# Forward substitution one hop later, up-weight loads and output stores on the sync queue, and the up-weight copies tied behind the output copies

## The chip, the cores and the metric

The kernel runs on one core of one Trainium2 chip. The metric is device time in microseconds; the kernel before was timed three times, with a median of 1085.12 us (1085.11 to 1085.61). Five engines work side by side: TensorE (PE, matmuls, with its weight loads shown as PEld), VectorE (DVE), ScalarE (ACT), GpSimd (POOL) and SyncE (SP), which issues most of the DMA transfers. ACT can issue transfers too; such issues stand in ACT's own instruction order.

## The reference

One layer of a decoder trunk on 512 tokens of width 2048:

```
h = RMSNorm(x);  z = h @ W_in          # r,k,v,decay and rate inputs | gate | pool input | pool gate
w = exp(-exp(-softplus(-(w0 + tanh(wd) @ W_up)) - 0.5));  a = sigmoid(a0 + ad @ A_up)
S_t = S_{t-1} (diag(w_t) - kk_t^T (a_t * kk_t)) + v_t^T k_t;  y_t = S_t r_t    # 16 heads of 64
y = GroupNorm per head (y) + bonus;  pool = windowed means, per-group linear map
x += concat(y, pool) * SiLU(gate) @ W_out
x += sigmoid(x @ W_pg + b_pg) * (p @ W_ple);  out = RMSNorm(x)
```

All in float32. The kernel reaches that accuracy with TensorE's float32r format by splitting each operand into a high part and a remainder and doing three matmuls (high x high, low x high, high x low) in `mm3` (L157).

## The kernel before, in words

**Dense work.** Weights come in 256 KB blocks: SP loads `raw_*`, ACT copies it to `whi_*` (L132), DVE subtracts to get `wlo_*` (L133). Blocks of columns give `zk`, `zr`, `zv`, `zg` (one per head pair) and `zb` (pool). These matmuls form a long stream that `pump` hands out in units of three; they fill TensorE between the small matmuls of the recurrence. After the stage of head pairs follow W_out (`acc_o`), the gate and the embedding (`acc_g`), and the last norm.

**Head pairs.** The 16 heads are treated as 8 pairs j of 128 columns, and the 512 tokens as 8 chunks of 64. The main loop does, for each j, `prepare(j+1)`, `recur(j)` and `gather(j+1)`.

- `decay_and_rate(j)` (L519) is called at the start of `gather(j-1)`. It takes the raw up-weights ur and ar, which `load_ab(j)` (L347, transfers at L354) has loaded, and makes PE's operands: ACT copies ur to us (L524) and its other half to uaz (L525), DVE subtracts to put the remainder in half of us (L526), and the same for as. PE then does pu and pa, whose results ACT turns into sig and tha. Each of us, as and uaz is one buffer, used again for the next j.
- `prepare(j)` builds the tiles ar and bk on DVE and stores bk to DRAM (bkd, L610). At its start it calls `load_ab(j+1)`. `scores(j)` does the chunk products (pm, masked to mt) and a bonus term (pbo, from kph and kpl), sends a part of mt to DRAM (nd, L651), reads it back as n (L656) and gathers bk as bg (L662).
- `invert(j)` (L668) is forward substitution in 31 steps of two DVE instructions, tm (L674) and an addition into xw (L678). The first step waits for n. At the end SP stores xw (xd, L682) and loads it back as x (L689).
- `recur(j)` runs the 8 chunks in 23 hops. A hop is a matmul, a DVE or ACT result (zs, uv, sbd) and some dense units. `step()` counts the hops; beyond hop HS it draws HN steps of `invert(j+1)` and ties them behind the last of these DVE results (`lead`). `between` stands after chunk 0 and holds `scores(j+1)`. After the last chunk, 32 small py<-uv,mt matmuls end the outputs, and ACT copies py to ysb (L847). DVE then takes statistics of ysb (L862, L864) and starts a reciprocal root with ve (L867) and rs (L143).
- The output yo is multiplied by the gate sg and stored to yd by ACT's queue (L893); the pool group's sgp goes the same way (L438).

**What sets the order.** PE's order in this stage is that of the program text. The order on DVE, ACT, SP and POOL is worked out by a scheduler with its own costs when the program is built; `tc.issue_after(x)` ties what follows it behind instruction x, and `tc.high_priority` moves an instruction up. At run time each engine goes through its list in that order.

With HS = 5 and HN = 2 the 31 steps fall on hops 6 to 20, two each, the last on hop 21, where the xd stores are issued too.

Of the kernel before, what the change touches and what calls it, by code (L numbers as in the profile page):

```python
# [21 lines left out]
NJ = DR // P  # L22
# [12 lines left out]
def trunk_kernel(ctx: ExitStack, tc: tile.TileContext, x, p, norm_g, w_in, mu, w0, w_up, a0, a_up,  # L35
                 k_k, k_a, r_k, ln_w, ln_b, w_pool, pool_scale, w_out, w_ple, w_pg, b_pg, final_g, out):
    nc = tc.nc
    PSUM = bass.MemoryType.PSUM
    x, p, w_in, w_out, w_ple, w_pg = x[0], p[0, 0], w_in[0], w_out[0], w_ple[0], w_pg[0]
    out = out[0]  # L40
# [146 lines left out]
    yd = dram.tile([KT, P, T], F32, name="yd", bufs=1)  # L187
# [5 lines left out]
    n_ = 0  # L193
# [154 lines left out]
    def load_ab(j):  # L348
        jc = slice(j * P, (j + 1) * P)
        w2 = []  # L350
        for nm, src in (("u", w_up), ("a", a_up)):
            raw = rw.tile([P, P], F32, name=f"{nm}r{j}", tag=f"l{nm}r")
            for h in range(2):
                nc.scalar.dma_start(out=raw[64 * h:64 * h + 64, :], in_=src[0, :, jc])  # L354
            w2.append((raw, rw.tile([P, P], F32R, name=f"{nm}s{j}", tag=f"l{nm}s")))
        wab[j] = w2

# [47 lines left out]
    def pool_unit(n):  # L405
        g, i = n // 4, n % 2
        win = WINDOWS[g]
        ps = psA.tile([P, T], F32, name=f"zb{n}", tag="acc")
        yield from zcols(ps, f"b{n}")
        if n % 4 < 2:  # L410
            u_ = pp.tile([P, T], F32, name=f"u{n}", tag="u")
            nc.scalar.copy(u_, ps)
            s_ = u_
            w_ = 1
            while w_ < win:
                n_ = pp.tile([P, T], F32, name=f"sw{n}_{w_}", tag="sw")
                nc.vector.tensor_tensor(n_[:, w_:T], s_[:, w_:T], s_[:, 0:T - w_], ALU.add)
                nc.vector.tensor_copy(n_[:, 0:w_], s_[:, 0:w_])
                s_, w_ = n_, 2 * w_
            nc.vector.tensor_tensor(s_[:, 0:win], s_[:, 0:win], rc[g], ALU.mult)  # L420
            nc.vector.scalar_tensor_tensor(u_, s_, 1.0 / win, u_, ALU.mult, ALU.subtract)
            if i == 0:
                dhl[g] = (pp.tile([P, 2, T], F32R, name=f"dh{g}", tag="dh", bufs=1),
                          pp.tile([P, 2, T], F32R, name=f"dl{g}", tag="dl", bufs=1))
            dh, dl = dhl[g]
            split(dh[:, i, :], dl[:, i, :], u_)
            return
        dh, dl = dhl[g]
        sgp = pp.tile([P, T], F32, name=f"sgp{n}", tag="sgp", bufs=1)
        silu2(ps, sgp)  # L430
        pq = psM.tile([P, T], F32, name=f"pp{n}", tag="m")
        wh, wl = chunk(f"wp{n}", 0)
        for k in range(2):
            mm3(pq, wh[:, k, :], wl[:, k, :], dh[:, k, :], dl[:, k, :], k == 0, k == 1)
            yield 0
        m = 2 * g + i
        nc.vector.scalar_tensor_tensor(sgp, pq, dp(73, m), sgp, ALU.mult, ALU.mult)
        nc.scalar.dma_start(out=yd[NJ + m], in_=sgp)  # L438

    phl, pn = [], []  # L440

# [74 lines left out]

    H1, H2, H3, H4, H5, HE = 6, 12, 20, 8, 13, 40

    def decay_and_rate(j):  # L519

        (ur, us), (ar_, as_) = wab.pop(j)
        for raw, st, z_, lo, hi in ((ur, us, uaz[0], slice(64, 128), slice(0, 64)),
                                    (ar_, as_, uaz[1], slice(0, 64), slice(64, 128))):
            nc.scalar.copy(st, raw)  # L524
            nc.scalar.copy(z_[hi, :], raw[hi, :])  # L525
            nc.vector.tensor_tensor(st[lo, :], raw[lo, :], st[lo, :].bitcast(F32), ALU.subtract)  # L526

        ps = psM.tile([P, T], F32, name=f"pu{j}", tag="m")
        mm(ps, us, uhh, start=True, stop=False)
        mm(ps, uaz[0], lal, start=False, stop=True)  # L530
        sig = rw.tile([P, T], F32, name=f"sig{j}", tag="t", bufs=4)
        nc.scalar.activation(sig, ps, AF.Tanh, scale=0.5, bias=dp(81, j))
        nc.vector.tensor_scalar(sig, sig, 0.5, 0.5, ALU.mult, ALU.add)
        nc.vector.tensor_tensor_scan(sig, seg, sig, 0.0, ALU.mult, ALU.add)
        pw = rw.tile([P, NCH, C + 1], F32, name=f"pw{j}", tag="pw", bufs=2)
        ipw = rw.tile([P, NCH, C], F32, name=f"ipw{j}", tag="ipw")
        nc.gpsimd.memset(pw[:, :, 0:1], 1.0)
        sig3 = sig.rearrange("p (c t) -> p c t", t=C)
        nc.scalar.activation(pw[:, :, 1:C + 1], sig3, AF.Exp, scale=-KAPPA)
        nc.scalar.activation(ipw, sig3, AF.Exp, scale=KAPPA)  # L540


        ps = psM.tile([P, T], F32, name=f"pa{j}", tag="m")
        mm(ps, as_, ahh, start=True, stop=False)
        mm(ps, uaz[1], lal, start=False, stop=True)
        tha = rw.tile([P, T], F32, name=f"tha{j}", tag="tha")
        nc.scalar.activation(tha, ps, AF.Tanh, scale=0.5, bias=dp(25, j))
        pws[j] = (pw, ipw, tha)
# [28 lines left out]
    def prepare(j):  # L577
        k_, r_, v_ = need("k", j), need("r", j), need("v", j)
        pw, ipw, tha = pws.pop(j)
        kk = kks.pop(j)  # L580
        if j + 1 < NJ:
            load_ab(j + 1)


        ar = rw.tile([P, NCH // 2, 4, C], F32, name=f"ar{j}", tag="ar", bufs=2)
        bk = rw.tile([P, NCH // 2, 4, C], F32, name=f"bk{j}", tag="bk")
        k4 = kk.rearrange("p (q c t) -> p q c t", c=2, t=C)
        pw4 = pw.rearrange("p (q c) t -> p q c t", c=2)
        i4 = ipw.rearrange("p (q c) t -> p q c t", c=2)
        kp = rw.tile([P, T], F32, name=f"kp{j}", tag="kp")  # L590
        nc.vector.tensor_scalar(kp, tha, dp(33, j), dp(41, j), ALU.mult, ALU.add)
        nc.vector.tensor_tensor(kp, kp, k_, ALU.mult)
        nc.vector.tensor_scalar(tha, tha, 0.5, 0.5, ALU.mult, ALU.add)
        nc.vector.tensor_tensor(ar[:, :, 0::3, :], r_.rearrange("p (q c t) -> p q c t", c=2, t=C),
                                pw4[:, :, :, 1:C + 1], ALU.mult)
        nc.vector.tensor_tensor(bk[:, :, 0::3, :], kp.rearrange("p (q c t) -> p q c t", c=2, t=C), i4, ALU.mult)
        nc.vector.scalar_tensor_tensor(ar[:, :, 1:3, :], k_.rearrange("p (q c t) -> p q c t", c=2, t=C), dp(89, j),
                                       pw4[:, :, :, 0:C], ALU.mult, ALU.mult)
        nc.vector.tensor_tensor(kk, kk, tha, ALU.mult)
        made = nc.vector.tensor_tensor(bk[:, :, 1:3, :], k4, i4, ALU.mult)  # L600
        with tc.issue_after(made.ins):
            nc.vector.scalar_tensor_tensor(kp, r_, dp(49, j), kp, ALU.mult, ALU.mult)
            if gates:
                gates.pop()()
        kph = rw.tile([P, T], F32R, name=f"kph{j}", tag="t", bufs=4)
        kpl = rw.tile([P, T], F32R, name=f"kpl{j}", tag="t", bufs=4)
        split(kph, kpl, kp)

        bkd = dram.tile([P, NCH * P], F32, name=f"bkd{j}", tag="bkd")
        nc.sync.dma_start(out=bkd, in_=bk.rearrange("p q s c -> p (q s c)"))  # L610
        st_[j] = dict(pw=pw, ar=ar, bk=bk, bkd=bkd, v_=v_, kp=(kph, kpl))
# [8 lines left out]
    def scores(j):  # L620
# [26 lines left out]
        for par in range(2):  # L647
            pb = 64 * (1 - par)
            for b in range(2):
                rows = slice(pb + 32 * b, pb + 32 * b + 32)  # L650
                nc.sync.dma_start(out=nd[par, b].rearrange("u r c -> r u c"),  # L651
                                  in_=mt[rows, par, :, 1 - par, 32 * b:32 * b + 32])
        nb = []
        for i in range(2):
            t_ = rw.tile([P, 16, 32], F32, name=f"n32{j}_{i}", tag=("kk", "kp")[i])
            n_ = nc.sync.dma_start(out=t_, in_=nd[:, :, :, 16 * i:16 * i + 16, :].rearrange(  # L656
                "a b u r c -> (a b u) r c").unsqueeze(0).to_broadcast([4, 32, 16, 32]))
            nb.append(t_)
        bg = rw.tile([P, NCH, 4, 32], F32, name=f"bg{j}", tag="bk")
        with tc.issue_after(n_.ins):  # L660
            for q in range(4):
# [105 lines left out]
    def recur(j, work, between):  # L767
        d = st_.pop(j)
        pw, ar, mt, bv, uv, mv, x1 = (d[n_] for n_ in ("pw", "ar", "mt", "bv", "uv", "mv", "x1"))
        hop = [0]  # L770
# [4 lines left out]
        def step():  # L775
            hop[0] += 1
            if hop[0] > HS:
                with tc.issue_after(lead[0].ins):
                    for _ in range(HN):
                        next(work, None)  # L780


        ysb = rw.tile([P, NT, P], F32, name=f"ysb{j}", tag="t", bufs=4)
        pys = {}
        for ch in range(NCH):
# [47 lines left out]
            if ch == NCH - 1:  # L833
                for c0 in range(0, NCH, 4):
# [9 lines left out]
                    py4 = py.rearrange("p (s c) -> p s c", c=P)  # L844
                    for pr in range(2):
                        yr = slice(64 * pr, 64 * pr + 64)
                        nc.scalar.copy(ysb[yr, c0 // 2:c0 // 2 + 2, :], py4[yr, pr::2, :])  # L847
            step()
            if ch == 0:
                between()  # L850
# [31 lines left out]
        def finish():  # L882
# [7 lines left out]
            def gate_out():  # L890
                nc.vector.tensor_tensor(yo, yo, bv, ALU.add)
                nc.vector.tensor_tensor(yo, yo, sg, ALU.mult)
                nc.scalar.dma_start(out=yd[j], in_=yo)  # L893

            return gate_out

        pending.append(finish)

    HC, HT, HX = (6, 9, 9), 130, 13
    HS, HN = 5, 2  # L900
    HP = 1000
    pending, normed, gates = [], [], []
    need("k", 0)
# [308 lines left out]
```

## Time and profile before

| what | value |
|---|---|
| timed runs, median | 1085.12 us (1085.11 to 1085.61) |
| profiled execution, its own time | 1082.7 us |
| its span | 1081.0 us, granted clock 0.998 |
| TensorE busy | 1056.6 us |
| DVE / ACT / POOL busy | 714.0 / 441.5 / 75.0 us |
| bytes moved by DMA | 146.94 MB, 136 GB/s mean |

The times of instructions all come from one profiled execution, which took 1082.7 us, 2.4 us less than the median of the timed runs. A row of a timeline reads: start in us, length in us, engine, line, operation, output tile <- input tiles, shapes, how many instructions the row holds, and in brackets how long the engine stood idle before it and what ended that. A row of a group reads: line, engine, operation, count, then shortest/median/longest in ns and the first and last start. Rows named SPq or ACTq are the issue of a transfer, not the transfer.

### The profile page before, as it was taken

How to read it: one execution, taken by the hardware profiler on the slowest of the kernel's cores; microseconds unless marked ns; L12 is line 12 of the kernel's file. 1: busy time of each engine (PE TensorE's matmuls, PEld its weight loads, DVE VectorE, ACT ScalarE, POOL GpSimd, SP SyncE). 2: the span in 40 equal slices, each digit the busy share in tenths (PEclk: the TensorE clock that was granted, in tenths of full speed). 3: DMA queues.
4: the chain of work that ended last, by engine and by line, in shares of the span. 5: the costliest groups of instructions: out<-in, count | busy, mean ns of one | idle time of the engine just before them, and what ended most of it. 6: DMA issues, size and time to landing. Idle time of an engine off the chain costs nothing.

```text
span 1081.0 us, 17106 instructions
## 1 busy us (share of the span) xinstructions
PE 1056.6 (98%) x5996; PEld 872.1 (81%) x5996; DVE 714.0 (66%) x1851; ACT 441.5 (41%) x901; POOL 75.0 (7%) x180
## 2 busy tenths in 40 slices
PE   5999999999999999999999999999999999999996
PEld 4888878888888887878788788888888888888885
DVE  6676978888779789787887857563432424445356
ACT  7633435335335354353352344553222222333337
POOL 2100010110110100200101201000000000000000
PEclk9999999999999999999999999999999999999999
DMA  7434443342634533434435343774434428355434
GB/s 236 117 115 111 139 116 88 116 120 74 168 88 114 144 89 105 120 89 112 106 91 158 100 129 111 239 243 141 171 121 143 166 98 271 122 182 161 169 98 156
DMA packets 212916, 146.94 MB, mean 136 GB/s; under 512 B 68085, under 2 KB 173150, under 8 KB 212830
## 3 DMA queue, kind: packets, MB, share of 16 engines
q1 hardware_dynamic: 192126, 112.28, 35.9%
q10 hardware_dynamic: 20704, 33.56, 9.4%
q8 instruction: 47, 0.77, 0.3%
q14 instruction: 39, 0.32, 0.1%
HBM read 122.21 MB, written 23.07 MB: 134 GB/s over the span
## 4 chain that ended last, share of the span: by engine, by line
PE 91%; DVE 4%; DMA 3%; ACT 2%; issue 1%; ACTq 0%; SPq 0%; DVEq 0%
PE acc_o L157 16%; PE acc_g L157 16%; PE zb L157 14%; PE zv L157 8%; PE zg L157 8%; PE zr L157 8%; PE zk L157 7%; PE py L157 2%; PE pu L157 2%; PE pple L157 2%; PE pm L157 1%; DMA n<-nd 1%; PE pp L157 1%; PE ps L157 1%; DMA xt<-in_x_dram 1%; PE pmv L157 1%
## 5 line engine op out<-in xcount | busy, mean ns | idle before, releaser
L133 DVE TENSOR_TENSOR wlo_g<-raw_g,whi_g 128x512 fp32r<-128x512 f32 x84 | 57.0, 685 | 74.4 <-ACT whi_g L132 72.3
L157 PE MATMUL zb<-hhi,whi_b 128*128 128x512 f32 x256 | 106.0, 414 | 0.0
L133 DVE TENSOR_TENSOR wlo_o<-raw_o,whi_o 128x512 fp32r<-128x512 f32 x64 | 43.9, 690 | 90.9 <-ACT whi_o L132 90.8
L157 PE MATMUL zb<-hhi,wlo_b 128*128 128x512 f32 x256 | 100.4, 392 | 0.0
L157 PE MATMUL acc_o<-whi_o,ylo 128*128 128x512 f32 x256 | 100.2, 391 | 0.0
L157 PE MATMUL acc_o<-whi_o,yhi 128*128 128x512 f32 x256 | 99.9, 390 | 0.0
L157 PE MATMUL zb<-hlo,whi_b 128*128 128x512 f32 x256 | 99.8, 390 | 0.0
L157 PE MATMUL acc_o<-wlo_o,yhi 128*128 128x512 f32 x256 | 99.7, 389 | 0.0
L132 ACT CAST whi_g<-raw_g 128x512 fp32r<-128x512 f32 x84 | 52.0, 621 | 105.3 <-PE acc_g L157 58.9
L157 PE MATMUL acc_g<-whi_g,x2hi 128*128 128x512 f32 x208 | 81.2, 391 | 0.0
L832 POOL TENSOR_SCALAR s0p<-sbd,pw 64x64 f32<-64x64 f32 x96 | 58.0, 604 | 332.0 <-DVE sbd L825 243.5
L157 PE MATMUL acc_g<-wlo_g,x2hi 128*128 128x512 f32 x208 | 80.9, 389 | 0.0
L157 PE MATMUL acc_g<-whi_g,x2lo 128*128 128x512 f32 x208 | 80.6, 389 | 0.0
L132 ACT CAST whi_o<-raw_o 128x512 fp32r<-128x512 f32 x64 | 39.9, 623 | 96.3 <-PE acc_o L157 96.3
L132 ACT CAST whi_b<-raw_b 128x512 fp32r<-128x512 f32 x64 | 39.7, 621 | 86.7 <-PE zb L157 29.2
L133 DVE TENSOR_TENSOR wlo_b<-raw_b,whi_b 128x512 fp32r<-128x512 f32 x64 | 43.6, 683 | 27.3 <-ACT whi_b L132 27.1
L157 PEld LDWEIGHTS zb<-hhi,wlo_b 128*128 128x128 f32 x256 | 48.0, 188 | 10.9
L678 DVE TENSOR_TENSOR xw<-xw,tm 128x60 f32<-128x60 f32 (+24 forms) x248 | 52.1, 210 | 7.0
L157 PEld LDWEIGHTS acc_o<-wlo_o,yhi 128*128 128x128 f32 x256 | 48.1, 188 | 9.9
L157 PEld LDWEIGHTS acc_o<-whi_o,ylo 128*128 128x128 f32 x256 | 48.1, 188 | 9.8
L157 PEld LDWEIGHTS acc_o<-whi_o,yhi 128*128 128x128 f32 x256 | 48.1, 188 | 9.7
L157 PEld LDWEIGHTS zb<-hhi,whi_b 128*128 128x128 f32 x256 | 48.2, 188 | 8.3
(283 smaller groups left out, 2529.6 us busy)
## 6 DMA issues: line engine op xcount, KB each, us to landing
raw_b<-in_w_in_dram SPq DMA_DIRECT2D x64, 256.0 KB
raw_o<-in_w_out_dram SPq DMA_DIRECT2D x64, 256.0 KB
raw_g<-in_w_pg_dram SPq DMA_DIRECT2D x64, 256.0 KB
raw_k<-in_w_in_dram SPq DMA_DIRECT2D x32, 256.0 KB
raw_r<-in_w_in_dram SPq DMA_DIRECT2D x32, 256.0 KB
raw_v<-in_w_in_dram SPq DMA_DIRECT2D x32, 256.0 KB
raw_g<-in_w_in_dram SPq DMA_DIRECT2D x32, 256.0 KB
bkd<-bk SPq DMA_DIRECT2D x8, 512.0 KB
```

What stands on the lines that cost most here:

```text
L132: nc.scalar.copy(hi, raw)
L133: nc.vector.tensor_tensor(lo, raw, hi.bitcast(F32), ALU.subtract)
L157: i = nc.tensor.matmul(*a, **k)
L678: nc.vector.tensor_tensor(xw[:, 0:n_, s + 1:32], xw[:, 0:n_, s + 1:32], tm[:, 0:n_, 0:w_], ALU.add)
L832: nc.gpsimd.tensor_scalar(s0p[hc, :], nxt[hc, hc], pcn[hc], None, ALU.mult)
```

## The change

Four edits:

1. HS goes from 5 to 6, and hop HE1 = 21 takes three steps. The 31 steps now fall on hops 7 to 20, two each, and three on hop 21; the xd stores are issued at hop 22.
2. `load_ab` and both yd stores go through the sync queue (SP) in place of ACT's.
3. `load_ab(j+1)` is called in `scores(j)`, tied behind the n loads, and no longer at the start of `prepare(j)`.
4. The four ACT copies of `decay_and_rate` are tied behind `tail`, the last ysb copy that has been issued by then. For j = 0 and 1 there is none yet.

```diff
 def load_ab(j):
-                nc.scalar.dma_start(out=raw[64 * h:64 * h + 64, :], in_=src[0, :, jc])
+                nc.sync.dma_start(out=raw[64 * h:64 * h + 64, :], in_=src[0, :, jc])
...
-        nc.scalar.dma_start(out=yd[NJ + m], in_=sgp)
+        nc.sync.dma_start(out=yd[NJ + m], in_=sgp)
...
+    tail = []
+
 def decay_and_rate(j):
-            nc.scalar.copy(st, raw)
-            nc.scalar.copy(z_[hi, :], raw[hi, :])
+            with tc.issue_after(tail[0].ins) if tail else ExitStack():
+                nc.scalar.copy(st, raw)
+                nc.scalar.copy(z_[hi, :], raw[hi, :])
             nc.vector.tensor_tensor(st[lo, :], raw[lo, :], st[lo, :].bitcast(F32), ALU.subtract)
...
 def prepare(j):
-        if j + 1 < NJ:
-            load_ab(j + 1)
...
 def scores(j):
+        if j + 1 < NJ:
+            with tc.issue_after(n_.ins):
+                load_ab(j + 1)
         bg = rw.tile([P, NCH, 4, 32], F32, name=f"bg{j}", tag="bk")
...
 def step():
-                    for _ in range(HN):
+                    for _ in range(HN + (hop[0] == HE1)):
...
-                        nc.scalar.copy(ysb[yr, c0 // 2:c0 // 2 + 2, :], py4[yr, pr::2, :])
+                        tail[:] = [nc.scalar.copy(ysb[yr, c0 // 2:c0 // 2 + 2, :], py4[yr, pr::2, :])]
...
 def gate_out():
-                nc.scalar.dma_start(out=yd[j], in_=yo)
+                nc.sync.dma_start(out=yd[j], in_=yo)
...
-    HS, HN = 5, 2
+    HS, HN, HE1 = 6, 2, 21
```

Three places show how the lists of the engines change. The first is ACT at the end of the recurrence of pair 1, around the pu and pa matmuls of pair 3 (a name's digits are the pair; what follows a last underscore is a buffer number; lines behind the first edits stand four later in the changed file). Before:

```order
L847 COPY ysb1_2614<-py1_0_2615 64x256 x2
L137 CAST kqh3_3320<-kk3_3318 128x512
L847 COPY ysb1_2614<-py1_4_2970 64x256 x2
L132 CAST whi_b2_3_1878<-raw_b2_3_1876 128x512
L369 ACTIVATE sv3_3355<-zv3_3130,dprm_133 128x512
L532 ACTIVATE sig3_3333<-pu3_3330,dprm_133 128x512
L547 ACTIVATE tha3_3345<-pa3_3342,dprm_133 128x512
```

And now:

```order
L851 COPY ysb1_2606<-py1_0_2607 64x256 x2
L137 CAST kqh3_3320<-kk3_3318 128x512
L851 COPY ysb1_2606<-py1_4_2966 64x256 x2
L527 CAST us3_2722<-ur3_2719 128x128
L528 CAST uaz0_570<-ur3_2719 64x128
L527 CAST as3_2726<-ar3_2723 128x128
L528 CAST uaz1_571<-ar3_2723 64x128
L132 CAST whi_b2_3_1871<-raw_b2_3_1869 128x512
L369 ACTIVATE sv3_3355<-zv3_3126,dprm_133 128x512
L535 ACTIVATE sig3_3333<-pu3_3330,dprm_133 128x512
```

The four copies for pair 3 now stand between the second ysb copies and whi_b; before they stood behind the pu and pa of the pair ahead.

The second is DVE at the same place. Before:

```order
L862 BN_STATS st1_3285<-ysb1_2614 128x6 x4
L864 BN_AGGR mvr1_3286<-st1_3285 128x2 x4
L138 TENSOR_TENSOR kql3_3321<-kk3_3318,kqh3_3320 128x512
L867 TENSOR_SCALAR ve81_3304<-mvr1_3286 128x8
L133 TENSOR_TENSOR wlo_b2_3_1879<-raw_b2_3_1876,whi_b2_3_1878 128x512
L143 TENSOR_SCALAR rs81_3303<-ve81_3304 128x8
```

(The two rows of the second half's statistics, which read like the first two, stand between kql3 and ve81.) And now, from the second half's statistics on:

```order
L866 BN_STATS st1_3285<-ysb1_2606 128x6 x4
L868 BN_AGGR mvr1_3286<-st1_3285 128x2 x4
L529 TENSOR_TENSOR us3_2722<-ur3_2719,us3_2722 64x128
L871 TENSOR_SCALAR ve81_3304<-mvr1_3286 128x8
L133 TENSOR_TENSOR wlo_b2_3_1872<-raw_b2_3_1869,whi_b2_3_1871 128x512
L143 TENSOR_SCALAR rs81_3303<-ve81_3304 128x8
L529 TENSOR_TENSOR as3_2726<-ar3_2723,as3_2726 64x128
```

The subtract for us3 stands behind the second aggregate, and that for as3 behind wlo_b and rs.

The third is DVE where the substitution for pair 6 begins, in the recurrence of pair 5. Before:

```order
L799 TENSOR_TENSOR zs0_568<-py5_0_6085,mv5_6033 64x128
L133 TENSOR_TENSOR wlo_r7_3_3580<-raw_r7_3_3577,whi_r7_3_3579 128x512
L674 TENSOR_TENSOR tm6_6224<-i32_116,n326_0_6163 128x31
L370 SCALAR_TENSOR_TENSOR sk7_6230<-zk7_6115,prm_131,sk7_6230 128x511
L678 TENSOR_TENSOR xw6_6223<-xw6_6223,tm6_6224 128x31
L674 TENSOR_TENSOR tm6_6224<-xw6_6223,n326_0_6163 128x30
L678 TENSOR_TENSOR xw6_6223<-xw6_6223,tm6_6224 128x30
L674 TENSOR_TENSOR tm6_6224<-xw6_6223,n326_0_6163 128x29
L678 TENSOR_TENSOR xw6_6223<-xw6_6223,tm6_6224 128x29
L674 TENSOR_TENSOR tm6_6224<-xw6_6223,n326_0_6163 128x28
L678 TENSOR_TENSOR xw6_6223<-xw6_6223,tm6_6224 128x28
L133 TENSOR_TENSOR wlo_v7_0_3586<-raw_v7_0_3583,whi_v7_0_3585 128x512
```

And now:

```order
L803 TENSOR_TENSOR zs0_568<-py5_0_6077,mv5_6033 64x128
L133 TENSOR_TENSOR wlo_r7_3_3572<-raw_r7_3_3569,whi_r7_3_3571 128x512
L370 SCALAR_TENSOR_TENSOR sk7_6223<-zk7_6107,prm_131,sk7_6223 128x511
L678 TENSOR_TENSOR tm6_6238<-i32_116,n326_0_6155 128x31
L682 TENSOR_TENSOR xw6_6237<-xw6_6237,tm6_6238 128x31
L678 TENSOR_TENSOR tm6_6238<-xw6_6237,n326_0_6155 128x30
L682 TENSOR_TENSOR xw6_6237<-xw6_6237,tm6_6238 128x30
L133 TENSOR_TENSOR wlo_v7_0_3578<-raw_v7_0_3575,whi_v7_0_3577 128x512
L829 SCALAR_TENSOR_TENSOR sbd1_567<-ps5_2_6253,pw5_5193,s0p5_1_6209 64x64 x2
```

Two steps in place of four stand ahead of wlo_v7 and of sbd1, and sk7 stands ahead of the first of them. In the list before, sbd1 follows wlo_v7 too.

## The prediction, made before the changed kernel was run

> **What bounds the kernel now.** I began with the page's first table, where TensorE (PE) is busy for nearly the whole span.
>
> ```profile
> PE 1056.6 (98%) x5996; PEld 872.1 (81%) x5996; DVE 714.0 (66%) x1851; ACT 441.5 (41%) x901; POOL 75.0 (7%) x180
> ```
>
> Next I took the table of 60 us windows (columns: window, length, then the busy time of PE, PEld, DVE, ACT and POOL, TensorE's granted clock, DMA share, GB/s), to see where PE is not busy in the head-pair stage, which runs up to about 700 us.
>
> ```profile
> 420.00:480.00 60.00, 59.07 (x326) 48.04 (x325) 46.71 (x156) 24.07 (x53) 8.77 (x14) 1.00 0.44 116
> 480.00:540.00 60.00, 58.02 (x382) 47.72 (x381) 48.94 (x135) 21.44 (x47) 6.50 (x14) 1.00 0.42 108
> 540.00:600.00 60.00, 59.48 (x412) 48.68 (x411) 48.44 (x136) 24.79 (x53) 6.97 (x10) 1.00 0.46 123
> ```
>
> These three windows miss 0.93 + 1.98 + 0.52 = 3.4 us; every other window of the stage misses less than 0.5. The waits view names what PE waited for (total us, times, longest).
>
> ```profile
> PE py L157 <- DVE sbd L825: 1.4, 2, 0.9
> PE px L157 <- issue: 1.1, 1, 1.1
> PE pu L157 <- DVE zs L799: 1.0, 2, 0.6
> PE pbo L157 <- DVE kpl L138: 0.3, 1, 0.3
> ```
>
> Together 3.8 us, about the same hole. A matmul's shown end overlaps the next one, so a stop costs a little more than its idle time. The longest run of dense matmuls in the chain of waits gives the true pitch:
>
> ```profile
> 83.27 10.88 PE zk L157 x48
> ```
>
> 10.88 / 48 = 0.227 us. Start to start against that pitch, the stops between 120 and 700 us sum to about 6.5 us (an estimate from the rows of that stretch). So this stage can give at most 6.5 us, 0.6% of the time, while any new wait in front of PE costs its full length, because PE's order is pinned and it has no spare time to catch up.
>
> **The change part by part.**
>
> *The tied copies (added wait).* `decay_and_rate(j)` makes PE's operand us of two steps: ACT copies ur, then DVE subtracts. Before, both ran some 50 us ahead of their use. Now the four ACT copies stand right behind the two ysb copies of the head pair whose end comes just before the pu matmul, and DVE's subtract stands behind the statistics made from those ysb rows. PE's order there is as before: nine dense matmuls after the last py, then pu. So each place is a race between nine matmuls (9 x 0.227 = 2.0 us) and copy, statistics, subtract. Here is the trace of before at j=3, DVE first, then ACT, then PE:
>
> ```profile
> 254.38 0.36 DVE L864 BATCH_NORM_AGGREGATE mvr<-st 128x2 f32<-128x6 f32 x4
> 254.78 0.17 DVE L867 TENSOR_SCALAR ve<-mvr 128x8 f32<-128x8 f32 x1
> 254.89 0.69 DVE L133 TENSOR_TENSOR wlo_b<-raw_b,whi_b 128x512 fp32r<-128x512 f32 x1
> 255.50 0.16 DVE L143 TENSOR_SCALAR rs<-ve 128x8 int32<-128x8 int32 x1
> ```
>
> ```profile
> 253.08 0.74 ACT L847 COPY ysb<-py 64x256 f32<-64x256 f32 x2
> 254.22 0.62 ACT L132 CAST whi_b<-raw_b 128x512 fp32r<-128x512 f32 x1 [0.39 <-ACT ysb L847]
> ```
>
> ```profile
> 254.21 0.39 PE L157 MATMUL pu<-uhh,us 128*128 128x512 f32 x1
> ...
> 254.66 0.39 PE L157 MATMUL pa<-ahh,as 128*128 128x512 f32 x1
> ```
>
> The subtract, and the pitch of the small ACT copies:
>
> ```profile
> L526 DVE TENSOR_TENSOR us<-ur,us x8: 289/289/290, 40.5 to 474.2; 64x128 fp32r<-64x128 f32 x8
> ```
>
> ```profile
> 187.10 0.30 ACT L525 CAST uaz<-ur 64x128 fp32r<-64x128 f32 x1
> 187.30 0.29 ACT L524 CAST as<-ar 128x128 fp32r<-128x128 f32 x1
> ```
>
> At j=3 the ACT copy of us would run from about 253.85 to 254.15, in time for pu at 254.21. But the subtract takes ve's slot at 254.78 and ends at 255.07; with some 0.06 to the next engine pu starts at 255.13, **0.92 later**. Then pa: the four copies, at 0.2 to 0.3 each, end near 254.87, so whi_b moves from 254.22 to 254.89; DVE, in its new order, runs us, ve, wlo_b (needs whi_b, 255.56 to 256.25), rs (0.1), as (0.27, to 256.64). pa starts at 256.70 instead of 254.66, **2.04 later** in all. j=5 and j=7 have the same rows in both orders: three places at about 2.05.
>
> At j=2 and j=6 the `as` subtract stands right behind ve, with no weight split between:
>
> ```profile
> 181.75 0.39 PE L157 MATMUL pu<-uhh,us 128*128 128x512 f32 x1
> ```
>
> ```profile
> 182.33 0.17 DVE L867 TENSOR_SCALAR ve<-mvr 128x8 f32<-128x8 f32 x1
> ```
>
> ```profile
> 473.27 0.39 PE L157 MATMUL pu<-uhh,us 128*128 128x512 f32 x1
> ```
>
> ```profile
> 473.84 0.17 DVE L867 TENSOR_SCALAR ve<-mvr 128x8 f32<-128x8 f32 x1
> ```
>
> us ends 0.29 after ve's old start: pu at 182.68 (+0.93) and 474.19 (+0.92); as ends about 0.45 later, just behind pa's new place, so **0.97** each. At j=4 a key split and ve stand ahead of us:
>
> ```profile
> 326.87 0.39 PE L157 MATMUL pu<-uhh,us 128*128 128x512 f32 x1
> ```
>
> ```profile
> 327.30 0.66 DVE L138 TENSOR_TENSOR kql<-kk,kqh 128x512 fp32r<-128x512 f32 x1
> ...
> 328.07 0.29 DVE L526 TENSOR_TENSOR us<-ur,us 64x128 fp32r<-64x128 f32 x1
> ```
>
> The subtract keeps its row place, now in front of pu: pu at 328.42, **+1.55**. Added: 3 x 2.05 + 2 x 0.97 + 1.55 = **9.6 us**. The lower end takes only the pu waits, 5 x 0.92 + 1.55 = 6.1 (if whi_b or the copies come sooner); the upper, 11, lets every pa cost as at j=3 (5 x 2.05 would be 10.3) with something on top at j=4.
>
> That DVE does not pass a waiting instruction rests on these rows: at 90.16 a substitution step had idled 5.09 us for its matrix, although whi_r was done at 89.14 and wlo_r, the next in the order, needed nothing else.
>
> ```profile
> 88.52 0.62 ACT L132 CAST whi_r<-raw_r 128x512 fp32r<-128x512 f32 x1 [2.05 <-PE zk L157]
> ```
>
> ```profile
> 90.16 0.19 DVE L674 TENSOR_TENSOR tm<-i,n 128x31 f32<-128x31 f32 x1 [5.09 <-DMA n<-nd]
> ...
> 91.91 0.68 DVE L133 TENSOR_TENSOR wlo_r<-raw_r,whi_r 128x512 fp32r<-128x512 f32 x1
> ```
>
> The Trainium skill says the same ("TensorE: Matmul & The Clock Gate", section "Architectural detail: the array is 16× 32×32, not 1× 128×128"): ACT and DVE queues are strict FIFO and PE may only pull weight loads forward, so neither the subtract nor the dense matmuls behind pu can step over the wait. If DVE could take whatever is ready, the subtract would run before the aggregate, at about 254.4, and j=3 would lose about 0.6 instead of 2.04; by that rule it cannot, and the rows above agree.
>
> *The substitution a hop later.* The steps of `invert` stand in DVE's order, and the first waits for its matrix from DRAM. What queues behind it is sbd, and PE waits for sbd:
>
> ```profile
> 512.26 0.19 DVE L674 TENSOR_TENSOR tm<-i,n 128x31 f32<-128x31 f32 x1 [2.21 <-DMA n<-nd]
> ```
>
> ```profile
> 515.85 0.49 PE L157 MATMUL py<-sbd,ar 128*128 128x128 f32 x2 [0.87 <-DVE sbd L825]
> ```
>
> With two steps instead of four ahead of sbd, two pairs of 0.45 us go from its front, and the shifted-copy row sk moves ahead of the wait: more than 0.87. The two sbd waits (1.4 by the waits view, 1.9 start to start with the smaller ones of their kind) go. The third step in the 15th hop is another pair of 0.4; it lies behind a wait of the same hop and only moves the xd stores, whose data the next head pair wants one hop, some 3 us, later. I price it at 0, bound 0 to 0.5.
>
> *The ACT queue freed.* The yd store and the up-weight loads leave ACT, where the issuing instruction waits for its operand:
>
> ```profile
> 425.17 0.32 ACTq L893 DMA_DIRECT2D yd<-yo  x1
> 425.54 0.60 ACT L373 ACTIVATE sg<-zg 128x512 f32<-128x512 f32 x1 [1.55 <-PE pbo L157]
> ```
>
> ACT then does sg and kph without that block, and the subtract in front of the mask products leaves DVE's list there:
>
> ```profile
> 425.67 0.27 DVE L526 TENSOR_TENSOR as<-ar,as 64x128 fp32r<-64x128 f32 x1
> ```
>
> That shortens the waits for kpl and zs, and perhaps the one at px. I credit 2 us of the remaining 4.6 (6.5 - 1.9), bounds 0 and 4.6. On SP, the store stands between two weight loads that are issued ahead of use; the up-weight issues go behind the n loads, in front of the bg gathers:
>
> ```profile
> L354 ACTq DMA_DIRECT2D ur<-in_w_up_dram x16: 472/496/620, 35.9 to 405.4; - x16
> ```
>
> Four issues at 0.5 to 0.6 are 2.2 us ahead of bg, whose transposed copy is used only when the next head pair starts, tens of us later: 0. Should that cover fail, it costs those 2.2 us once per head pair.
>
> *Sum.* +9.6 - 1.9 - 2.0 = +5.7, taken as **+5.6 us**, with ends 6.1 - 6.5 = -0.4 and 11 - 1.9 = +9.1. The profiled execution took 1082.7 (span 1081.0), so 1088.3 in its terms; the median of the timed runs is 2.4 above it, hence **1090.7**.
>
> **The rivals.**
>
> *R1, it cancels.* The new waits are only the 0.92 of each pu (6.1 in all), and PE's six stops let DVE and ACT run ahead, so that all 6.5 us of old stops vanish. Net -0.4: about 1084.7. For it: while PE stands, the others catch up, and most old stops are below 1 us. Against: the stops at 425 to 430, 486 and 515 us lie tens of us from a pu place, and the lead gained is used up by DVE, which is busy for four fifths of these windows.
>
> *R2, faster.* The chip lets the statistics end sooner than I read, say because the ysb copies follow their py with ACT no longer held by stores: the subtract would have to come 0.9 us sooner. Then the tie costs 0.2 per place, 1.2 in all, and 5.7 of old stops vanish: -4.5, 1080.6. It decides from the point where the second aggregate ends before pu's old start less 0.35. Against: at j=3 the ysb row starts with no idle time noted behind kqh, ACT's own work, and no store is near it. The Trainium skill ("DMA: Bandwidth & Descriptors", section "Issuing engines are not separate DMA queues") says that another issuing engine saves no more than the time of issuing; the 0.5 us issue row above is of that size.
>
> *R3, more is lost.* The late sig and tha push the decay chain, x1 comes a hop late, and no old stop goes: +9.6 and another wait of about 1 us at pq in two head pairs: +11.6, 1096.7. For it: DVE is the engine with the least slack. Against: in every pair PE's own delay of 0.9 or more precedes that place.
>
> **How the numbers follow.** Forecast 0.68, with its own range 1087 to 1093.5; R1 0.14; R2 0.08; R3 0.10. A change below 0.2% (2.2 us) can't be told from none here. Faster by more: R2, 0.08. Same: R1, 0.14. Slower: forecast and R3, 0.78. The range takes the forecast's ends (-0.4 and +9.1) and thereby R1: 1084.5 to 1094.7, leaving out R2 and most of R3.
>
> **What would show it.** In the changed profile PE's waits view should get rows pu <- DVE us of about 0.9 (1.5 at j=4) at six places, and pa <- DVE as of about 1.1 at three; the row py <- DVE sbd should go, and kpl and zs shrink. The windows up to 600 us should each miss 1 to 2 us of PE. If pu has no wait for us, the subtract was not behind the statistics in time and the main term is wrong; if py <- sbd stays, the substitution's term is.

## The result and the profile after

The changed kernel takes 1092.58 us (median of six runs, 1090.85 to 1095.52) beside 1085.2 us for the kernel before in the same runs. The ratio is 1.0067, with a 95% interval of 1.0053 to 1.0081: 5.7 to 8.8 us slower, 7.3 in the middle. The forecast was 1090.7, with a range of 1084.5 to 1094.7. The profiled execution took 1091.91 us with a span of 1090.2, 9.2 us above the profile of before.

First the busy times and then the waits of PE in the profile after:

```profile
PE 1058.1 (97%) x5996; PEld 870.7 (80%) x5996; DVE 716.4 (66%) x1851; ACT 440.0 (40%) x901; POOL 75.1 (7%) x180
```

```profile
PE pu L157 <- DVE us L529: 5.1, 6, 1.4
...
PE pa L157 <- DVE ve L144: 2.4, 3, 0.8
PE py L157 <- DVE sbd L829: 1.6, 4, 0.8
PE pu L157 <- DVE zs L803: 1.0, 3, 0.4
```

PE's work is the same; the span grew by waits. Two rows are new: pu waits for us at six places, pa at three. They are 7.5 us of idle time, 9.0 from start to start, and 9.9 with the matmuls right behind the stops, which come late too (below). The rows for sbd and zs are still there, 1.6 and 1.0 where the profile of before had 1.4 and 1.0.

Here is pair 3's place: ACT, DVE and PE in the profile after.

```profile
255.89 0.30 ACT L527 CAST us<-ur 128x128 fp32r<-128x128 f32 x1
...
256.93 0.62 ACT L132 CAST whi_b<-raw_b 128x512 fp32r<-128x512 f32 x1
```

```profile
256.42 0.36 DVE L868 BATCH_NORM_AGGREGATE mvr<-st 128x2 f32<-128x6 f32 x4
256.81 0.29 DVE L529 TENSOR_TENSOR us<-ur,us 64x128 fp32r<-64x128 f32 x1
257.13 0.17 DVE L871 TENSOR_SCALAR ve<-mvr 128x8 f32<-128x8 f32 x1
257.58 0.69 DVE L133 TENSOR_TENSOR wlo_b<-raw_b,whi_b 128x512 fp32r<-128x512 f32 x1 [0.28 <-ACT whi_b L132]
258.19 0.16 DVE L143 TENSOR_SCALAR rs<-ve 128x8 int32<-128x8 int32 x1
258.26 0.28 DVE L529 TENSOR_TENSOR as<-ar,as 64x128 fp32r<-64x128 f32 x1
```

```profile
256.01 0.40 PE L157 MATMUL zv<-hhi,wlo_v 128*128 128x512 f32 x1
257.15 0.50 PE L157 MATMUL pu<-uhh,us 128*128 128x512 f32 x1 [0.75 <-DVE us L529]
257.49 0.39 PE L157 MATMUL pu<-lal,uaz 128*128 128x512 f32 x1
258.68 0.47 PE L157 MATMUL pa<-ahh,as 128*128 128x512 f32 x1 [0.80 <-DVE ve L144]
...
259.22 0.60 PE L161 MATMUL pv<-ident,sv 128*128 128x128 f32 x4
```

ACT's copy of us is ready at 256.19, but DVE subtracts only after the aggregate, at 256.81, and pu starts 0.05 after its end. The subtract for as follows wlo_b, which has waited for whi_b behind the four copies. The row names ve as what pa waited for; as itself ends at 258.54, just before pa's start.

The second pu starts 0.34 us behind the first, not 0.23, and the second pa 0.31 behind its first. So a stop costs about 0.1 us more than the start of the waiting matmul shows. The whole place is therefore read from the last dense matmul to the first pv behind pa: 256.01 to 259.22 here, 3.21 us. In the profile of before it was 1.15 us:

```profile
253.97 0.40 PE L157 MATMUL zv<-hhi,wlo_v 128*128 128x512 f32 x1
...
255.12 0.60 PE L161 MATMUL pv<-ident,sv 128*128 128x128 f32 x4
```

The stops of PE from start to start, against the 0.227 us pitch:

| place | prediction | profile after |
|---|---|---|
| pu, j=2, 3, 5, 6, 7 | 0.93, 0.92, 0.92, 0.92, 0.92 | 0.92, 0.92, 0.92, 0.92, 0.89 |
| pu, j=4 | 1.55 | 1.55 |
| pa, j=3, 5, 7 | 1.13 each | 0.96, 0.97, 0.96 |
| sum of these, with 0.05 forecast for pa at j=2, 6 | 9.6 | 9.0 |
| whole place, j=2 to 7 in order | 0.97, 2.05, 1.55, 2.05, 0.97, 2.05 | 1.04, 2.06, 1.66, 2.07, 1.03, 2.04 |
| sum of the whole places | 9.6 | 9.9 |
| py for sbd, whole stage | 0.4 left of 2.3 | 2.3 |
| pu for zs, px, pbo | about 2 of 4.2 left | 2.8 |
| W_out, first operand | 0 | 0.56 |

In the table by windows (120 to 180 us and on), the two slices that hold j=3 and j=4 miss 2.4 and 1.4 us of PE, where before they were full:

```profile
240.00:300.00 60.00, 57.62 (x402) 46.79 (x401) 47.01 (x132) 24.67 (x54) 5.89 (x11) 1.00 0.39 106
300.00:360.00 60.00, 58.62 (x409) 48.16 (x408) 52.11 (x157) 26.43 (x58) 9.00 (x12) 1.00 0.41 111
```

So the loss is where it was forecast. The 9.9 us of the six places, the 0.6 at W_out, and the 1.4 that the row pu for zs, px, pbo gave back make 9.1 of the 9.2 us by which the span grew. What did not come is most of the gain. Theories for that: the longer wait of the first substitution step for its matrix n has come with the up-weight loads, now issued right behind n (theory N); or n's time varies anyway (theory V); and ACT was not the limit at the places where its freedom was to pay.

### The profile page after: what moved, and what is told of

Read it like the earlier page. It is cut to its first block, busy times and chain, and to the rows that moved or that the text cites. A ratio compares the mean times of both kernels' runs of the same rounds, so it can differ in the third digit from the quotient of the medians.

```text
span 1090.2 us, 17103 instructions
## 1 busy us (share of the span) xinstructions
PE 1058.1 (97%) x5996; PEld 870.7 (80%) x5996; DVE 716.4 (66%) x1851; ACT 440.0 (40%) x901; POOL 75.1 (7%) x180
## 4 chain that ended last, share of the span: by engine, by line
PE 86%; DMA 5%; DVE 4%; ACT 3%; issue 1%; SPq 0%; ACTq 0%; DVEq 0%
PE acc_g L157 16%; PE acc_o L157 15%; PE zb L157 13%; PE zr L157 8%; PE zv L157 8%; PE zg L157 7%; PE zk L157 6%; PE pple L157 2%; PE py L157 2%; DMA yin<-yd 2%; PE pm L157 1%; PE pu L157 1%; DMA ur<-in_w_up_dram 1%; PE ps L157 1%; DMA xt<-in_x_dram 1%
```

## The experiments

| kernel | median us | ratio to before, 95% interval |
|---|---|---|
| the changed kernel | 1092.58 | 1.0067 (1.0053 to 1.0081) |
| before, tie alone | 1094.52 | 1.0095 (1.0080 to 1.0110) |
| changed, tied behind uv | 1082.07 | 0.9968 (0.9957 to 0.9980) |
| changed, no tie | 1115.97 | 1.0299 (1.0277 to 1.0322) |
| before, HS = 6 alone | 1082.89 | 0.9984 (0.9974 to 0.9993) |
| before, HS = 7 alone | 1080.76 | 0.9957 (0.9943 to 0.9972) |
| changed, no tie, loads behind bg | 1085.82 | 1.0009 (0.9997 to 1.0020) |
| before, yd stores on sync alone | 1086.02 | 1.0002 (0.9991 to 1.0013) |
| changed, no tie, loads in the old place | 1083.03 | 0.9985 (0.9976 to 0.9995) |
| the same with HS = 7 | 1081.66 | 0.9966 (0.9954 to 0.9978) |
| changed, tied behind uv, HS = 7 | 1081.05 | 0.9961 (0.9947 to 0.9976) |

The kernel before lay between 1084.5 and 1085.4 us in these comparisons, so ratios are compared, not medians.

### The tie alone

```diff
 # the kernel before, and
+            with tc.issue_after(tail[0].ins) if tail else ExitStack():
+                nc.scalar.copy(st, raw)
+                nc.scalar.copy(z_[hi, :], raw[hi, :])
...
+                        tail[:] = [nc.scalar.copy(ysb[yr, c0 // 2:c0 // 2 + 2, :], py4[yr, pr::2, :])]
```

> The kernel before with the tie alone: hops, queues and the place of the loads as before. Theory T: pu waits of 0.9 at j=2, 3, 5, 6, 7 and 1.55 at j=4, pa waits of 0.96 at j=3, 5, 7: +9.0 us, near 1094, and the old waits of PE for sbd (1.9 us from start to start at 441, 516 and 590 us) are still there. Rival R1 (the six stops let DVE and ACT run ahead and take the old waits away): +2.5 to +4, 1088 to 1089. Theory Q: no more than half of +9, below 1090.

Measured: 1094.52, 0.95% or 10.3 us above the kernel before (8.7 to 11.9). The waits of PE in its profile:

```profile
PE pu L157 <- DVE us L529: 5.1, 6, 1.4
PE py L157 <- DVE sbd L828: 3.4, 4, 1.6
...
PE pa L157 <- DVE ve L144: 2.4, 3, 0.8
```

The two rows for us and ve are those of the changed kernel to the digit, 9.0 us from start to start and 9.9 for the whole places, and the sbd waits are not smaller: 4.6 us from start to start. R1, by which the six stops let the other engines run ahead and take the old waits away, has fallen.

### The same tie one place earlier

```diff
 # the changed kernel, but
-                    nc.scalar.copy(uv[pb:pb + 64, ch, hc], psu[hc, hc])
+                    u_ = nc.scalar.copy(uv[pb:pb + 64, ch, hc], psu[hc, hc])
+            tail[:] = [u_]
...
-                        tail[:] = [nc.scalar.copy(ysb[yr, c0 // 2:c0 // 2 + 2, :], py4[yr, pr::2, :])]
+                        nc.scalar.copy(ysb[yr, c0 // 2:c0 // 2 + 2, :], py4[yr, pr::2, :])
```

> The changed kernel with the copies tied behind the last chunk's uv copies in place of the ysb copies; all else as changed. DVE's subtracts for us and as now stand ahead of the statistics of ysb. Theory T (the loss is DVE's subtract standing behind these statistics, not the tie as such): no wait of pu or pa, 9.0 us less than the changed kernel: 1083.5, with the sbd waits of PE still near 2 us. Rival (any tie of this kind costs, because four copies of 0.2 us now stand in front of ysb, the key split and the next weight split): PE waits by 0.8 us or more at other places of each pair, and the time stays above 1087.

Measured: 1082.07, 0.32% below the kernel before and 1% below the changed one. The subtracts for pair 3 stand ahead of the statistics (DVE, then PE):

```profile
249.98 0.29 DVE L529 TENSOR_TENSOR us<-ur,us 64x128 fp32r<-64x128 f32 x1
...
250.39 0.28 DVE L529 TENSOR_TENSOR as<-ar,as 64x128 fp32r<-64x128 f32 x1
...
254.63 0.36 DVE L869 BATCH_NORM_AGGREGATE mvr<-st 128x2 f32<-128x6 f32 x4
```

```profile
254.22 0.40 PE L157 MATMUL zv<-hhi,wlo_v 128*128 128x512 f32 x1
254.46 0.39 PE L157 MATMUL pu<-uhh,us 128*128 128x512 f32 x1
```

pu follows the dense matmul by 0.24 us: no wait, at any pair. So the cost is the place to which the tie behind ysb brings the two subtracts, behind the statistics and (for as) behind a weight split that has waited for ACT, and not a tie as such. The difference to the changed kernel is about 10.7 us (1.0067 less 0.9968), beside the 9.9 us of the six places; the intervals of the two ratios are wider than what is left between them.

### No tie at all

```diff
 # the changed kernel, but
-            with tc.issue_after(tail[0].ins) if tail else ExitStack():
-                nc.scalar.copy(st, raw)
-                nc.scalar.copy(z_[hi, :], raw[hi, :])
+            nc.scalar.copy(st, raw)
+            nc.scalar.copy(z_[hi, :], raw[hi, :])
```

> The changed kernel without the tie of the up-weight copies; the sync queue, the loads behind n and the later substitution stay. Theory T (the tie pays all of the loss): the six pu waits and three pa waits of the changed kernel, 9.0 us from start to start, vanish, so about 9 us below the changed kernel, near 1083.5; but the subtracts for us and as now stand between the first substitution steps and sbd, 0.56 us more ahead of sbd, so the sbd waits stay near 2.3 us or grow to 4, which leaves 1083.5 to 1085.5. Theory Q (the moved transfers pay a good part): the wait of the first substitution step for n stays long and the time stays above 1087. Theory S (PE loses the same elsewhere): 1090 or more, with new waits of PE that sum to the old.

Measured: 1115.97, 32 us above the kernel before (30 to 35), the slowest of all, which no theory had. The waits of ACT and of PE show a new one:

```profile
ACT uaz L527 <- DMA ur<-in_w_up_dram: 50.3, 7, 9.2
```

```profile
PE ps L157 <- ACT uv L816: 24.5, 6, 5.5
```

Pair 4's loads, in the recurrence of pair 2 (ACT, then PE):

```profile
309.90 0.30 ACT L527 CAST uaz<-ur 64x128 fp32r<-64x128 f32 x1 [9.18 <-DMA ur<-in_w_up_dram]
...
310.94 0.42 ACT L816 COPY uv<-pu 64x64 f32<-64x64 f32 x2
```

```profile
305.49 0.40 PE L157 MATMUL zk<-hhi,wlo_k 128*128 128x512 f32 x1
311.42 0.80 PE L157 MATMUL ps<-uv,bkn 128*128 128x128 f32 x2 [5.53 <-ACT uv L816]
```

With the loads issued behind n and nothing to hold the copies, the scheduler put the copies ahead of a uv copy, as if the loads had landed. They land 9 to 10 us after their issue, and uv, which PE needs, stands behind them on ACT. So the third edit (later loads) needs a tie of some kind, and my prediction did not see that it would cost some 32 us without one. In the profiled execution, 38 us longer than that of before, the six stops are 25.5 us from start to start; about 13 more (an estimate) are the stretches of 27 us in all behind them in which matmuls came at half pace (last section). The experiment thus doesn't say what the changed kernel is without the statistics' wait; the version tied behind uv does.

### The later substitution alone, and once more later

```diff
 # the kernel before, with
-                    for _ in range(HN):
+                    for _ in range(HN + (hop[0] == HE1)):
-    HS, HN = 5, 2
+    HS, HN, HE1 = 6, 2, 21
 # and the second one with
+    HS, HN, HE1 = 7, 2, (19, 20, 21)      # hop[0] in HE1
```

> The kernel before with the substitution a hop later alone (HS = 6, three steps in hop 21). My step of the prediction: the two large sbd waits go, -1.9 us, 1083.3, and the wait from the second issue of the n loads to the first step stays at its 5.0 to 5.5 us, since no transfer has moved. Rival (the hop does nothing, because the first step is still tied behind the same zs and its wait for n still stands ahead of sbd): the sbd waits stay at about 2 us and the time at 1085.2.

> The kernel before with the substitution one hop later still (HS = 7, three steps in hops 19, 20 and 21), so that the first step stands behind sbd of that chunk, and nothing waits for n ahead of it. Theory: the sbd waits that were left with HS = 6 (1.8 us) go, whatever the time that n takes: 1081, 1.8 us below HS = 6 and 3.5 below the kernel before. Rival (DVE's list is full later: three steps a hop delay zs, sbd or the last step, and with it the next pair's first matmuls): new waits of PE at zs, sbd or pq, 1083 or more.

Measured: 1082.89 (0.8 to 2.8 us less than before) and 1080.76 (3.0 to 6.2 less). By the ratio the first is 1.7 us, beside the 1.9 that were forecast. But its profile doesn't look as expected, since the wait for n stays ahead of sbd:

```profile
587.01 0.19 DVE L674 TENSOR_TENSOR tm<-i,n 128x31 f32<-128x31 f32 x1 [4.14 <-DMA n<-nd]
```

```profile
PE py L157 <- DVE sbd L825: 1.5, 2, 1.2
```

Here n took 7.0 us from the end of its second issue to the first step, where the profile of before had at most 5.5. Hop 7 is tied behind the same zs as hop 6, because `lead` is set only by zs and sbd, and hop 7 is that of a uv copy: a hop later took two steps from in front of sbd and left the first step where it was. With HS = 7 the first step stands behind sbd, and the wait is gone in all seven pairs of the main loop:

```profile
586.61 0.29 DVE L825 SCALAR_TENSOR_TENSOR sbd<-ps,pw,s0p 64x64 f32<-64x64 f32 x1
586.93 0.19 DVE L674 TENSOR_TENSOR tm<-i,n 128x31 f32<-128x31 f32 x1
```

The rival there, new waits at zs or pq, shows little: one stop of 0.66 us at a pq matmul near 410 us, which stands in the HS = 6 profile too.

### The kernel before once more, and the loads behind bg

These two ask why n took so long.

> The kernel before once more, for a second profile. Theory V (the time from the second n issue to the first step varies from one execution to the next by 1 to 2 us in single pairs, whatever stands on the queue): one or more pairs at 5.9 us or above, and with it other sbd waits of PE than the first profile showed. Theory N (the longer times come from the changed queues): all eight pairs again between 4.9 and 5.6 us, and sbd waits at the same three places.

Measured: one execution, 1085.98, a span of 1084.3. The last pair, DVE and then PE, and the row of the waits view:

```profile
589.97 0.19 DVE L674 TENSOR_TENSOR tm<-i,n 128x31 f32<-128x31 f32 x1 [3.69 <-DMA n<-nd]
```

```profile
593.49 0.49 PE L157 MATMUL py<-sbd,ar 128*128 128x128 f32 x2 [1.55 <-DVE sbd L825]
```

```profile
PE py L157 <- DVE sbd L825: 4.1, 5, 1.5
```

n took 6.55 us here and 5.3 to 6.0 at the other pairs; the sbd waits are 4.1 us where the first profile of the same kernel had 1.4. So theory V is right for this kernel: the first profile was an execution in which n came early.

```diff
 # the changed kernel without the tie, and
-        if j + 1 < NJ:
-            with tc.issue_after(n_.ins):
-                load_ab(j + 1)
...
-                nc.sync.dma_start(out=bg[32 * q:32 * q + 32],
+                b_ = nc.sync.dma_start(out=bg[32 * q:32 * q + 32],
...
+        if j + 1 < NJ:
+            with tc.issue_after(b_.ins):
+                load_ab(j + 1)
```

> The changed kernel without the tie, and with the up-weight loads issued behind the bg gathers instead of right behind the n loads. Theory N (the up-weight loads right behind n make n land later, 5.6 to 6.75 us from the second issue where the kernel before has 5.0 to 5.5): the time from issue to first step falls back to 5.0 to 5.5 us, the sbd waits of PE fall below 0.7 us in sum, and the time is 1.5 to 2 us below the same kernel with the loads right behind n: 1081 to 1082.5. Rival (the longer wait for n has another cause, such as the stores on the sync queue or the later start of the pair): the wait for n stays at 6 us or more in several pairs and the time at 1083.5 to 1085.

Measured: 1085.82, and n still took 7.2 and 7.0 us at pairs 3 and 4. Theory N falls as the cause of the long waits: they come with no transfer moved, and stay when the loads stand elsewhere. This kernel also lost 2.0 us at one place, 111 us, where pair 1's us and as came late for the first pu and pa.

Put together, by the number of hops alone (time from the end of the second n issue to the first step, mean and longest of the 8 pairs; stops of PE for sbd, from start to start and summed over the stage):

| execution | HS | n, mean | n, longest | stops for sbd |
|---|---|---|---|---|
| before, first profile | 5 | 5.2 | 5.5 | 2.3 |
| before, once more | 5 | 5.7 | 6.6 | 5.2 |
| tie alone | 5 | 5.5 | 6.6 | 4.6 |
| yd stores on sync alone | 5 | 5.8 | 6.9 | 5.4 |
| changed | 6 | 5.8 | 6.8 | 2.3 |
| HS = 6 alone | 6 | 5.7 | 7.0 | 1.8 |
| loads behind bg | 6 | 5.7 | 7.2 | 2.3 |
| tied behind uv | 6 | 5.9 | 6.6 | 2.0 |
| changed, no tie | 6 | 5.8 | 7.3 | 2.0 |
| loads in the old place | 6 | 5.4 | 6.3 | 1.1 |
| HS = 7 alone | 7 | no wait | no wait | 0.5 |
| old place, HS = 7 | 7 | no wait | no wait | 0.5 |
| tied behind uv, HS = 7 | 7 | no wait | no wait | 0.7 |

("No wait" is for pairs 1 to 7; the substitution of pair 0 stands ahead of the main loop and waits in every execution.) The stops go with HS: 4.6 to 5.4 us with HS = 5, 1.8 to 2.3 with 6 and 0.5 to 0.7 with 7. Two executions lie below their group, the first profile of before (2.3) and the loads in the old place (1.1). They are also the two with the shortest mean time of n, so what is left of the stops while the step still waits ahead of sbd seems to vary with n.

### The queues

```diff
 # the kernel before, with both yd stores
-        nc.scalar.dma_start(out=yd[NJ + m], in_=sgp)
+        nc.sync.dma_start(out=yd[NJ + m], in_=sgp)
...
-                nc.scalar.dma_start(out=yd[j], in_=yo)
+                nc.sync.dma_start(out=yd[j], in_=yo)
```

> The kernel before with the two kinds of yd stores on the sync queue alone. My step of the prediction (ACT freed, 2 us): the waits for kpl, zs near 430 and px shrink, 1083. Rival (the late stores stand behind weight loads on the sync queue, so that W_out's first operands come later): the gain is 0.5 to 1 and PE waits 0.6 to 1.3 us in front of W_out, 1084.5 to 1085.5.

Measured: 1086.02, a ratio of 1.0002: no change. The place near 425 us that I had taken for ACT blocked by its store (ACT, then PE):

```profile
428.60 0.60 ACT L373 ACTIVATE sg<-zg 128x512 f32<-128x512 f32 x1 [1.25 <-DVE yo L892]
```

```profile
429.16 0.50 PE L157 MATMUL pbo<-kpl,blk 128*128 128x512 f32 x1 [0.27 <-DVE kpl L138]
```

The store has left ACT's list, and ACT still stands idle 1.25 us before sg, for the multiplication yo x sg that reads the old sg (L892). In the profile of before this multiplication ended at 425.13, and the store was issued at 425.17:

```profile
424.46 0.67 DVE L892 TENSOR_TENSOR yo<-yo,sg 128x512 f32<-128x512 f32 x1
```

So the store had waited for the same multiplication, and cost ACT only its own issue, the 0.3 us by which 1.55 became 1.25. kpl is as late as before, and px's stop is 1.27. In front of W_out PE now stops 0.7 us, the rival's part.

> The changed kernel without the tie and with the up-weight loads back at the start of the pair's preparation, still on the sync queue; later substitution and yd stores as changed. It asks what the sync queue is worth when the copies stand 50 us ahead of their use, as in the kernel before. My step of the prediction (ACT freed of stores and loads, up to 2 us): 1 us or more below the kernel before with the later substitution alone (1082.9): 1081 to 1082. Rival (it is worth nothing, as with the stores alone): 1082.9 within 1 us. No wait of ACT for ur or ar above 1 us in either.

The edit: the changed kernel without the tie, with `load_ab(j + 1)` back at the start of `prepare(j)`, on the sync queue. Measured: 1083.03, beside 1082.89 for the same hops with all transfers on ACT. The sync queue is worth nothing here either.

> The last kernel with the substitution from hop 8 on as well. If the sync queue is worth 1 us and the second hop 1.8: 1079.5 to 1080.2. If the sync queue is worth nothing: 1080.8, the same as the kernel before with HS = 7.

> The changed kernel with the copies tied behind the uv copies and the substitution from hop 8 on (HS = 7, three steps in hops 19, 20 and 21): the two edits that have paid, together. If they add: the sbd waits left in the version with the uv tie (2.0 us) go, 1080.1 to 1080.5, 5 us below the kernel before. Rival (they share their gain, since the kernel before with HS = 7 alone is at 1080.8 and the freed ACT is worth nothing): 1080.8 or more.

Both with `HS, HN, HE1 = 7, 2, (19, 20, 21)`. Measured: 1081.66 and 1081.05, ratios of 0.9966 and 0.9961 beside the 0.9957 of the kernel before with HS = 7 alone, a difference within their intervals. Neither adds to it, and the kernel before with these two lines changed is the best version found: 0.43% below it (0.28 to 0.57).

## Why the prediction came out as it did

**The tied copies: right in mechanism, place and size.** Forecast 9.6 us at six pairs, measured 9.9 in the profile, with the pu stop to within 0.03 us at each of the six. What the sum left out is that the matmul behind a stop comes some 0.1 us late as well: j = 2, 4 and 6 cost 0.06 to 0.11 more than forecast. At j = 3, 5 and 7 this is hidden, since the pa stop was forecast 0.16 to 0.17 too long (0.96 for 1.13; DVE ended as 0.27 us behind wlo_b, where I had 0.39), and 2.04 to 2.07 came out for 2.05: two errors that cancel. That it is the subtract behind the statistics is shown by the tie moved to uv, which has no such wait. In timed runs the tie costs 10.3 us on its own.

**"The two sbd waits go": wrong in the profile, about right in the time.** The step "with two steps instead of four ahead of sbd, two pairs of 0.45 us go from its front ... more than 0.87" took n's arrival from one execution, as 5.0 to 5.5 us after its issue. It varies up to 7.2, and the wait for it is still ahead of sbd, since hop 7 hangs on the same zs as hop 6. The stops stayed at 2.3 us, as large as in the profile of before, which was a lucky one. Against the other executions with HS = 5 (4.6 to 5.4) they did shrink, and the edit alone gains 1.7 us where I had 1.9. That the two agree is luck: the 1.9 was to be all of a small sum, and the 1.7 is part of a larger one.

**"I credit 2 us" for the freed ACT queue: wrong.** The stores alone give 1.0002, the loads on the sync queue nothing either. The step that failed is the reading of the 1.55 us in front of sg as the store's doing; both waited for DVE's multiplication, and the store's own part was 0.3. In the changed profile the stop for kpl is gone and px went from 1.28 to 0.91, but the queue is not what did it: the kpl stop is gone with HS = 6 alone too, and px is back at 1.27 with the loads on the sync queue in their old place. What the queue did bring is the stop at W_out, 0.56, which I had at nothing.

**The sum.** Forecast +5.6. With the single terms as measured it is 10.3 for the tie, less 1.7 for the hop, plus 0 for the queues: 8.6, beside a measured 7.3 (5.7 to 8.8). The forecast was low because 2 us of gain that do not exist stood in it. That the profiled execution lay 2.4 us below the median was noted and added at the end; it was a sign of the early n: the second profile of the kernel before is 3.3 us longer, with 2.9 us more of sbd stops.

**The rivals.** R1 (it cancels) falls with the tie alone at +10.3 us. R2 (faster) asked for the second aggregate to end before pu's old start less 0.35; at pair 3 it ended at 256.78, and by the full pitch pu's place was 256.24, so it came 0.54 behind it, as in the profile of before (254.74 for 254.21). The version tied behind uv, whose subtracts don't wait for the statistics at all, is 3.5 us faster than before; 1.7 of that is the later hop, and what gives the rest isn't shown. R3's late x1 is not seen: no wait at pq in the changed profile. The 32 us of the loads without a tie were on no list.

## What to carry to other kernels

Where PE's order is pinned and full, the price of a tie is read by laying the new list of the slower engine over the old times: the last instruction of the chain that the tie now puts behind something else sets the loss, here a DVE subtract behind statistics and not the copy that was tied, and one place earlier the same tie is free. What a stop cost is read from where the dense matmuls go on at full pitch, not at the matmul that waited: here 9.9 us, not 9.0. A step that waits for a transfer should be ordered behind the result that PE waits for, not only fewer of its followers ahead of it, because the transfer's time varies by more than the followers cost. Terms taken from one profile whose time lies below the median are suspect in just the waits that vary; a second profile of the same kernel shows which.

## What the runs showed of the hardware

The clock: in the kernel without a tie, PE stood still for 5.5 us near 311 us. The windows before, in, just behind and after that stop (the granted clock is the number behind POOL's):

```profile
300.00:305.00 5.00, 5.00 (x25) 4.17 (x24) 2.15 (x5) 0.69 (x2) 1.26 (x2) 1.00 0.52 124
...
311.40:315.40 4.00, 3.98 (x10) 3.24 (x11) 2.64 (x10) 1.20 (x3) 1.44 (x2) 0.50 0.37 109
318.00:322.00 4.00, 4.00 (x21) 3.35 (x20) 2.43 (x8) 1.72 (x4) 0.65 (x1) 1.00 0.44 98
```

Half the clock was granted, and dense matmuls came every 0.43 us in place of 0.227. The Trainium skill ("TensorE: Matmul & The Clock Gate", section "What's actually happening") has this: half the clock after an idle window of about 3.4 us, full clock after about as long a busy one. The drop agrees with these rows; the return took longer here, about 6 us by the starts of the matmuls up to 317.4 us. Behind the six stops of this kernel it took between 2.9 and 6.0 us, and the clock fell behind the shortest of them too, 2.9 us idle (0.52 granted from 393 to 396 us).

What I had not expected is the same with far shorter stops. In the kernel with the tie alone, pair 5's stops of 0.75 and 0.80 us idle at 408.5 and 410.1 us, 3 us of which PE was busy for little more than half, were followed by this:

```profile
408.00:411.00 3.00, 1.68 (x7) 1.14 (x8) 2.49 (x15) 1.78 (x4) 0.00 (x0) 0.94 0.19 42
411.00:414.50 3.50, 3.50 (x12) 2.83 (x11) 3.50 (x10) 2.79 (x5) 0.00 (x0) 0.57 0.46 108
```

Six matmuls there cost 0.20 to 0.35 us more each, 1.4 us in all. The profile of the changed kernel, with the same two stops at the same place, kept the full clock. Its six timed executions had mean granted clocks of 0.998, 0.997, 0.997, 0.995, 0.995 and 0.994, and took 1090.85, 1091.39, 1091.91, 1093.24, 1094.80 and 1095.52 us, in that order. The 0.004 between the first and the last clock are worth 4.4 us of 1090 (an estimate), beside 4.7 between their times. That fits a tie that sometimes costs a stretch of clock beside its waits. The five timed executions of the tie alone don't show it: the slowest, 1096.12 us, has the highest clock, 0.998. And the price of the tie in timed runs (10.3, and 10.7 by the tie moved) is above the 9.9 us of its six places by less than the intervals, so it needs no such part. The drop behind short stops was seen at one place of one profile, and that it lengthens the timed runs is not shown.
